# Attention pieces between scores and turnings, norm weights in the rotary table, one-hot rows for seven experts

## Chip, core and metric

The kernel runs on one core of one Trainium2 chip. The time is the device time of the program in microseconds; before the change it is 1876.73 us, the median of three runs (1873.58 to 1881.66).

## What is computed

One layer of an encoder on 1024 tokens of 1024 features, all in float32. Three branches read `h = RMSNorm(x)` through one combined projection; their merged result goes through an output projection, and a mixture of 32 experts follows.

```python
h = _rmsnorm(x, g_mix[l]); proj = h @ w_in[l]
q_a, k_a, v_a, cx, cb, cc, q_m, gate_logits = jnp.split(proj, IN_SPLITS, axis=-1)
q_a = _partial_rope(_rmsnorm(q_a.reshape(b, s, 12, 64), g_qn_attn[l]), cos, sin)   # k_a likewise
# 3 head groups of 4 heads, (window, dilation) = (128,1), (512,4), (2048,16)
#   softmax over |i - j| <= half in each strided subsequence; groups combined by their lse
z_conv = cb * conv3(cc * cx)                       # depthwise, width 3
mkv = _rmsnorm(mem, g_mem[l]) @ w_mem_kv[l]        # 256 memory tokens, 4 heads of 128
k_m = _rmsnorm(k_m, g_kn_mem[l]); o_mem = softmax(q_m k_m / sqrt(128)) v_m
merged = sum(sigmoid(gate[i]) * (branch[i] @ w_proj[i]))
x = x + merged @ w_out[l]
h2 = _rmsnorm(x, g_ffn[l])
# best of 4 expert groups, best 2 of its 8 experts: ids, weights
x = x + sum over both (silu(h2 @ w_gate[e]) * (h2 @ w_up[e])) @ w_down[e] * weight
```

The rotation turns 16 of the 64 dimensions of a head (`ROT`); the norm weights of q and k are one vector of 64 each, the same for all heads.

## The kernel before

The order of the instructions on each engine is the order in which the program is written: the kernel schedules by hand, and an engine does its instructions in that order. Products of float32 matrices are made of three matmuls (`mm3`, lines 233 to 235): both operands are kept as a rounded part and a rest, made by a copy on ScalarE and a subtraction on VectorE (`split`). Weights of the dense part stream in through SyncE's queue (`WStream`, lines 82 and 83), five raw and eight split buffers; `ws.pump()` at a unit's end splits the next block.

PSUM has three pools: `mm` with four banks (`bank()`, products and scores), `tr` with two (`trb()`, everything that is turned by TensorE), `sm` with two (`smb()`, value products `po` and small things).

**Units.** `Emit` (line 112) writes the dense part as a row of units. `E.unit(fn)` runs one, counts it, and then runs what `E.later(n, fn)` asked for n units on; `E.ahead(n, fn)` puts a step ahead of the unit that comes n later. One attention group runs in `att_group(g, before, fillers, at)`: first eight q/k units (a token tile each: 24 matmuls, then `qk_chain`), then the `before` units, then the attention units of `att_units(g)` (15, 12 and 8 in groups 0, 1 and 2) with the fillers put ahead of the units named in `at`.

`qk_chain` normalizes a q/k tile: the sum of squares, then `qn` on VectorE (line 487), the weights `gqk` on GpSimd (490), the rotation by `cs` on GpSimd (496 to 499), and three or four units later `tp()` turns it (507) and evicts four pieces, two by ScalarE and two by VectorE.

An attention unit makes its scores (737, 768 or 799), then `softmax_unit`: VectorE adds the mask and takes the maximum (698), ScalarE the exponentials (705). Its `pv()`, `PVLAG` = 2 units later, turns the probabilities (`pT_of`, 712) and copies them by ScalarE to `pTs` (714); `fin()`, one unit after that, makes the value product (751, 782, 813).

In group 0 the `before` units are those of its own v (`v_units(0)`: four units of 24 matmuls, their turnings at 565), and after the first of them `att_consts` makes the masks, after the others `mem_rows` turns the memory tokens (633; split by lines 242 and 243 into `memT`). Its fillers are the four v units of group 1. Group 1 has the v units of group 2 ahead of it and four `mem_kv` units as fillers, group 2 gate units in pieces.

**Output projection.** Sixteen units of 24 matmuls, one per token tile and half; the residual row is turned (1634) after the matmuls of `kt == 3` of the next unit, and its router logits follow after `kt == 6`.

**Experts.** Each of the 32 experts has 128 slots (`CAP`). Its weights come in four or six pieces of 1 MB through SyncE (`XStream`, 1323) and are split into `xhl` (1350 by ScalarE, 1351 by VectorE), six chunks at most ahead. A step of the loop for expert e: `gate_e` (in its middle `actT_e(e - 1)` turns the last expert's activations), `xeT(e + 1)` turns the next expert's rows (1729), `down_e(e - 1)` with the output copy `ye` by ScalarE (1789, one buffer) and the scatter that adds it to `out` by GpSimd (1790), then `up_e(e)`. `gather(e)` fetches the rows of expert e by GpSimd (1576).

Which token has which slot is known in two ways. `slot_rows(pool, e, engs)` makes eight one-hot matrices `R` (1544), and `slots(e)` multiplies them with `aux` (nine matmuls into `slots`, 1563), from which VectorE works out the row numbers `idx` (1568) and, where asked, the weights `lw`. Before the change experts 0 to 4 (`NR` = 5) have their row numbers from there, and expert 0 its weights. The others read a table: `table_put(i, c)` scatters token numbers and weights (16 puts, 1521, on GpSimd), `table_get` reads it back (four reads, 1528, on GpSimd), `table_sum` adds the copies.

```python
    for e in range(NE):
        gate_e(e)
        if e + 1 < NE: xeT(e + 1)
        if e < 2:
            slots(e + 3, weights=False); gather(e + 3)
            table_part(4 * e, 4 * e + 4)
            if e == 0: slot_rows(moe, 4, (nc.vector,))
            else: table_get()
        elif 3 <= e < NE - 3: gather(e + 3)
        if 0 < e < NE - 1:
            if e == 2: table_sum(); gather(5)
            down_e(e - 1)
        up_e(e)
        if e == 0: slots(0, rows=False)
```

## Time and profile before

| | before |
|---|---|
| median of three runs | 1876.73 us (1873.58 to 1881.66) |
| the profiled execution | 1873.2 us |
| span from its first to its last instruction | 1871.4 us |
| TensorE matmuls | 1752.9 us, 94% of the span, 8194 |
| VectorE | 962.0 us, 51% |
| ScalarE | 820.4 us, 44% |
| GpSimd | 376.9 us, 20% |
| mean granted TensorE clock | 0.969 |
| HBM read | 277.97 MB, 163 GB/s with what is written |

One execution is profiled, and all durations come from it; busy time is the time in which an engine works on an instruction, and the rest of the span it waits. The granted clock is 1 at 2.4 GHz; a mean between 0.5 and 1 is a share of the stretch at 1.2 GHz. The attention part runs from about 26 to 425 us, the rest of the dense part to 1100, the output projection to about 1225, the experts to 1860. A row of waits names the waiting instruction, what ended the wait, and total, number and longest of such waits. In a timeline row the bracket holds the engine's idle time ahead of the instruction and what released it; an entry with xN joins N instructions in a row.

### The profile page before, as it was taken

The numbers are of one execution on the slowest core, as the hardware profiler recorded it, in microseconds if no ns is written. First come the engines' busy times: TensorE is split into PE (matmuls) and PEld (weight loads), VectorE is DVE, ScalarE is ACT, GpSimd is POOL, SyncE is SP. The second block draws the span as 40 slices with busy tenths as digits, with TensorE's granted clock in tenths as the row PEclk, the third lists the DMA queues.
The fourth block names the chain that finished last, engine by engine and source line by source line (L and its number), as shares of the span: only waits on it lengthen the run. The fifth ranks groups of instructions, "written<-read, shape, count | busy, mean of one in ns | idle before, by whom it ended". The sixth has DMA issues, their size and how long they took to land.

```text
span 1871.4 us, 22857 instructions
## 1 busy us (share of the span) xinstructions
PE 1752.9 (94%) x8194; PEld 1381.9 (74%) x8194; DVE 962.0 (51%) x1985; ACT 820.4 (44%) x1459; POOL 376.9 (20%) x526
## 2 busy tenths in 40 slices
PE   5988987989999999999999999968999999999995
PEld 4765865767788888888888878755777777777774
DVE  5733644651333243122652234785777777777773
ACT  6344234243212122121442224345777777777772
POOL 6500522410100000111324110054111111112110
PEclk9999998999899999999999999968999999999998
DMA  5110022021102121122011252668899999999981
GB/s 187 36 35 24 14 70 86 15 63 30 34 18 68 34 74 46 40 62 81 1 46 52 68 199 88 226 243 294 307 358 377 357 370 359 371 372 359 371 328 20
DMA packets 99666, 289.18 MB, mean 155 GB/s; under 512 B 14448, under 2 KB 60640, under 8 KB 74848
## 3 DMA queue, kind: packets, MB, share of 16 engines
q1 hardware_dynamic: 85456, 259.03, 36.9%
q0 software_dynamic: 11904, 24.48, 5.1%
q10 hardware_dynamic: 2192, 4.20, 0.6%
q8 instruction: 65, 1.06, 0.2%
q14 instruction: 49, 0.40, 0.1%
HBM read 277.97 MB, written 26.46 MB: 163 GB/s over the span
## 4 chain that ended last, share of the span: by engine, by line
PE 68%; DVE 4%; DMA 2%; ACT 2%; issue 2%; POOL 1%; SPq 0%; POOLq 0%; ACTq 0%; DVEq 0%
PE mmb L233 19%; PE mmb L235 19%; PE mmb L234 19%; PE mmb L1784 5%; PE trb L1729 1%; PE trb L1763 1%; PE mmb L910 1%; ACT pt L705 1%; PE po L1160 1%; PE mmb L1119 1%; DMA xw<-in_w_gate_dram 1%; DVE xhl L1351 1%; PE lgp L1641 0%; DVE whl L83 0%; POOL R L1544 0%
## 5 line engine op out<-in xcount | busy, mean ns | idle before, releaser
L1351 DVE TENSOR_TENSOR xhl<-xw,xhl 128x1024 fp32r<-128x1024 f32 x320 | 377.2, 1221 | 151.0 <-ACT xhl L1350 147.4
L1350 ACT ACTIVATE xhl<-xw 128x1024 fp32r<-128x1024 f32 x320 | 328.1, 1060 | 41.9 <-PE mmb L235 33.2
L233 PE MATMUL mmb<-hT,whl 128*128 128x512 f32 x768 | 305.9, 398 | 0.0
L235 PE MATMUL mmb<-hT,whl 128*128 128x512 f32 x768 | 301.8, 393 | 0.3 <-DVE whl L83 0.2
L234 PE MATMUL mmb<-hT,whl 128*128 128x512 f32 x768 | 301.5, 393 | 0.0
L233 PE MATMUL mmb<-xhl,xT 128*128 128x512 f32 x512 | 217.7, 425 | 6.7 <-ACT xhl L1350 6.7
L83 DVE TENSOR_TENSOR whl<-wraw,whl 128x512 fp32r<-128x512 f32 (+1 forms) x196 | 135.2, 707 | 158.6 <-ACT whl L82 153.7
L235 PE MATMUL mmb<-xhl,xT 128*128 128x512 f32 x512 | 202.7, 396 | 1.4 <-DVE xT L240 1.4
L234 PE MATMUL mmb<-xhl,xT 128*128 128x512 f32 x512 | 202.8, 396 | 0.5 <-DVE xhl L1351 0.5
L233 PEld LDWEIGHTS mmb<-hT,whl 128*128 128x128 f32 x768 | 146.1, 190 | 33.7 <-issue 2.7
L235 PEld LDWEIGHTS mmb<-hT,whl 128*128 128x128 f32 x768 | 145.7, 190 | 32.4 <-DVE whl L83 1.3
L234 PEld LDWEIGHTS mmb<-hT,whl 128*128 128x128 f32 x768 | 146.1, 190 | 29.4
L82 ACT ACTIVATE whl<-wraw 128x512 fp32r<-128x512 f32 (+1 forms) x196 | 115.4, 601 | 110.8 <-PE mmb L235 88.1
L994 POOL TENSOR_TENSOR merged<-merged,sg 128x512 f32<-128x512 f32 x32 | 41.3, 1292 | 461.2 <-DVE sg L993 461.1
L233 PEld LDWEIGHTS mmb<-xhl,xT 128*128 128x128 f32 x512 | 98.6, 192 | 32.8 <-issue 7.2
L234 PEld LDWEIGHTS mmb<-xhl,xT 128*128 128x128 f32 x512 | 98.0, 191 | 27.0 <-issue 7.2
L1784 PE MATMUL mmb<-xw,aT 128*128 128x512 f32 x256 | 115.0, 592 | 0.0
L235 PEld LDWEIGHTS mmb<-xhl,xT 128*128 128x128 f32 x512 | 97.8, 191 | 23.0 <-DVE xT L240 2.1
L1576 POOL DMA_INDIRECT xe<-hbuf,idx x32 | 53.0, 1656 | 286.8 <-PE trb L1729 260.5
L233 PE MATMUL mmb<-whl,hT 128*128 128x512 f32 x256 | 106.3, 415 | 1.2 <-ACT hT L242 1.1
L993 DVE TENSOR_TENSOR sg<-mmb,sg 128x512 f32<-128x512 f32 x32 | 22.1, 690 | 165.2 <-PE mmb L235 161.5
L235 PE MATMUL mmb<-whl,hT 128*128 128x512 f32 x256 | 101.1, 395 | 0.2
(378 smaller groups left out, 2813.2 us busy)
## 6 DMA issues: line engine op xcount, KB each, us to landing
xw<-in_w_down_dram SPq DMA_DIRECT2D x64, 1024.0 KB, 12.9
xw<-in_w_gate_dram SPq DMA_DIRECT2D x62, 1024.0 KB, 18.6
xw<-in_w_up_dram SPq DMA_DIRECT2D x62, 1024.0 KB, 14.0
wraw<-in_w_in_dram SPq DMA_DIRECT2D x68, 256.0 KB, 2.9
wraw<-in_w_in_dram SPq DMA_DIRECT2D x48, 192.0 KB, 3.0
wraw<-in_w_in_dram SPq DMA_DIRECT2D x48, 128.0 KB, 2.6
xt<-in_x_dram SPq DMA_DIRECT2D x8, 512.0 KB, 6.0
wraw<-in_w_mem_kv_dram SPq DMA_DIRECT2D x16, 256.0 KB, 3.3
```

Source lines behind the costliest of these rows:

```text
L82: self.nc.scalar.activation(t[:, 0, :n], r, AF.Copy)
L83: self.nc.vector.tensor_tensor(t[:, 1, :n], r, t[:, 0, :n].bitcast(F32), OP.subtract)
L233: nc.tensor.matmul(ps, lhsT=lh, rhs=rh, start=first, stop=False)
L234: nc.tensor.matmul(ps, lhsT=lh, rhs=rl, start=False, stop=False)
L235: nc.tensor.matmul(ps, lhsT=ll, rhs=rh, start=False, stop=last)
L705: nc.scalar.activation(pt[:, c], pt[:, c], AF.Exp, bias=nb[:, h:h + 1], scale=0.125, accum_out=sg[:, qt, 1, h0 + h:h0 + h + 1])
L993: nc.vector.tensor_tensor(sg, pp, sg, OP.mult)
L994: nc.gpsimd.tensor_tensor(m_, m_, sg, OP.add)
L1350: nc.scalar.activation(t[:, 0], src, AF.Copy)
L1351: nc.vector.tensor_tensor(t[:, 1], src, t[:, 0].bitcast(F32), OP.subtract)
L1576: nc.gpsimd.indirect_dma_start(out=xe[e % 2][:CAP], out_offset=None, in_=hbuf, in_offset=bass.IndirectOffsetOnAxis(ap=slot_i(e), axis=0), ...
L1784: nc.tensor.matmul(ps[h], lhsT=t[:, a], rhs=w[:, a, h * 512:(h + 1) * 512], start=False, stop=(a == 1))
```

## The change

- `E.later` gets `first=True`, which puts a step ahead of the others that are due; `E.ahead` and `PVLAG` go. `pv()` comes four units after the scores, `fin()` two units after that and first among what is due.
- The fillers of groups 0 and 1 are cut after kt = 1, 3 and 5 into pieces of six matmuls (`CUTS4`), sixteen a group, one piece ahead of an attention unit. The turnings of group 1's v come two and four units after their piece.
- `mem_rows` leaves the v units of group 0 and becomes four fillers of its own among the attention units; `att_consts` moves to the q/k unit of tile 4.
- The norm weights of q and k: the 16 rotated dimensions are multiplied into the rotary table (`csg`, on GpSimd at the start), the others are a scale per partition (`gcol`) in the evictions behind the turning, which become one instruction each for ScalarE and VectorE. Line 490 goes; the rotation is two products over q and k for four.
- The memory keys: their squares go from GpSimd to ScalarE, the product with `y` from GpSimd to VectorE, four units later, and the weight into the eviction.
- In the output projection the turning moves from kt 3 to kt 5, the logits from 6 to 7.
- Experts 0 to 6 have row numbers and weights from one-hot rows (`NR` = 7), all made on VectorE; those for the weights of experts 0 to 2 are made a second time. The puts are spread over steps 0 to 2 (6, 6, 4), behind the gather, and the table is read in step 3 and summed in step 4.

```diff
+    def later(self, n, fn, first=False):
+
+        self.q.insert(0 if first else len(self.q), (self.t + n, fn))
...
-    def ahead(self, n, fn):
-
-        self.a.append((self.t + n, fn))
...
+            for s in range(2):
+                for c, v in ((0, n2), (1, n1)):
+                    nc.gpsimd.tensor_tensor(
+                        csg[:, s, c].rearrange("p t (a e) -> p t a e", a=2),
+                        v[:, :, None, :].to_broadcast([P, NT, 2, 8]),
+                        gqk[:, s, 0:ROT].rearrange("p (a e) -> p a e", a=2)[:, None]
+                        .to_broadcast([P, NT, 2, 8]), OP.mult)
...
+    gqk = atc.tile([P, 2, ROT], F32, name="gqk")
+    gcol = atc.tile([P, 2], F32, name="gcol")
+    for s_, g_ in ((0, g_qn_attn), (1, g_kn_attn)):
+        nc.gpsimd.dma_start(gqk[:, s_], bc_rows(g_, ROT))
+        for h in range(2):
+            nc.gpsimd.dma_start(gcol[h * HD + ROT:(h + 1) * HD, s_:s_ + 1],
+                                g_[0, ROT:HD].rearrange("(p c) -> p c", c=1))
...
-        nc.gpsimd.tensor_tensor(qv, qv, gqk[:, :, None, :].to_broadcast([P, 2, 4, HD]), OP.mult)
...
-                        nc.scalar.activation(d, src, AF.Copy)
+                    nc.scalar.activation(d, src, AF.Copy, scale=gcol[:, 0:1])
...
+                if (g, t) == (0, 4):
+                    att_consts()
...
-                        E.later(1, tp(ct, q))
+                        E.later(2 * q + 2 if cuts else q + 1, tp(ct, q))
...
-                nc.gpsimd.tensor_tensor(sq, qn, qn, OP.mult)
+                nc.scalar.activation(sq, qn.rearrange("p h d -> p (h d)"), AF.Square)
-                nc.gpsimd.tensor_tensor(qn, qn, y[:, :, None].to_broadcast([P, 4, MH]), OP.mult)
-                nc.gpsimd.tensor_tensor(qn, qn, gkm[:, None, :].to_broadcast([P, 4, MH]), OP.mult)
+                def norm():
+                    nc.vector.tensor_tensor(qn, qn, y[:, :, None].to_broadcast([P, 4, MH]), OP.mult)
...
-                    E.later(1, fin)
-                E.ahead(PVLAG[g], pv)
+                    E.later(2, fin, True)
+                E.later(4, pv)
...
-    att_group(0, [first_v(i, u) for i, u in enumerate(v_units(0))],
-              v_units(1), [2, 5, 8, 11])
-    att_group(1, v_units(2), [mem_kv(k_, m_) for k_ in ("mk", "mv") for m_ in range(2)],
-              [1, 4, 7, 10])
+    CUTS4 = (1, 3, 5)
+    f0 = flat(v_units(1, CUTS4))
+    at0 = list(range(15)) + [14]
+    for kp, i in enumerate((2, 5, 8, 11)):
+        k = at0.index(i) + 1
+        f0.insert(k, lambda kp=kp: mem_rows(kp))
+        at0.insert(k, i)
+    att_group(0, flat(v_units(0)), f0, at0)
+    f1 = flat([mem_kv(k_, m_, CUTS4) for k_ in ("mk", "mv") for m_ in range(2)])
+    att_group(1, flat(v_units(2)), f1, sorted(list(range(12)) + [1, 4, 7, 10]))
...
-                    if kt == 3 and "tp" in late:
+                    if kt == 5 and "tp" in late:
...
-    slot_rows(moe, 0, (nc.gpsimd,))
-    slot_rows(moe, 3, (nc.gpsimd,))
...
+        if e < 4:
+            slot_rows(moe, e + 3, (nc.vector,))
+        elif e < NE - 3:
+            if e == 4:
+                table_sum()
             gather(e + 3)
         if 0 < e < NE - 1:
             down_e(e - 1)
+        if e < 4:
+            slots(e + 3)
+            gather(e + 3)
+        if e < 3:
+            slot_rows(moe, e, (nc.vector,))
+            table_part(*((0, 6), (6, 12), (12, 16))[e])
         up_e(e)
+        if e < 3:
+            slots(e, rows=False)
+        elif e == 3:
+            table_get()
```

TensorE's row among the units of group 0 before: L712 turns one unit's probabilities, L737 are scores, L751 a value product, L233 to L235 the start of a filler of 24 matmuls.

```order
L751 MATMUL po_1311<-pTs_1298,vv_1065 64x128 x4
L737 MATMUL mmb_1317<-kT_664,qT_663 128x256
L737 MATMUL mmb_1318<-kT_664,qT_663 128x256
L712 MATMUL trb_1328<-ident_93,pt_1304 128x128 x4
L737 MATMUL mmb_1335<-kT_664,qT_663 128x256
L737 MATMUL mmb_1336<-kT_664,qT_663 128x256
L751 MATMUL po_1346<-pTs_1333,vv_1065 64x128 x4
L712 MATMUL trb_1352<-ident_93,pt_1321 128x128 x4
L233 MATMUL mmb_1359<-hT0_107,whl_947 128x512
L234 MATMUL mmb_1359<-hT0_107,whl_947 128x512
L235 MATMUL mmb_1359<-hT0_107,whl_947 128x512
L233 MATMUL mmb_1359<-hT1_108,whl_947 128x512
```

The same place after the change: L724 turns, L226 to L228 are a piece of a filler, L749 scores, L763 a value product.

```order
L724 MATMUL trb_1319<-ident_93,pt_1267 128x128 x4
L226 MATMUL mmb_1249<-hT4_111,whl_1019 128x512
L227 MATMUL mmb_1249<-hT4_111,whl_1019 128x512
L228 MATMUL mmb_1249<-hT4_111,whl_1019 128x512
L226 MATMUL mmb_1249<-hT5_112,whl_1019 128x512
L227 MATMUL mmb_1249<-hT5_112,whl_1019 128x512
L228 MATMUL mmb_1249<-hT5_112,whl_1019 128x512
L749 MATMUL mmb_1332<-kT_661,qT_660 128x256
L749 MATMUL mmb_1333<-kT_661,qT_660 128x256
L763 MATMUL po_1343<-pTs_1324,vv_1025 64x128 x4
L226 MATMUL mmb_1249<-hT6_113,whl_1059 128x512
L227 MATMUL mmb_1249<-hT6_113,whl_1059 128x512
```

Six matmuls stand between a turning and the next scores, and between a value product and the next turning, where turning, scores and value product stood next to each other for two units at a time.

GpSimd's row at the start of the experts before: the last four table puts (L1521), the table reads (L1528), and the first two scatters (L1790) and the gathers behind them (L1576).

```order
L1521 DMA tab_d0_89<-tsrc_7829,tdst_7830 4096x2
L1521 DMA tab_d1_90<-tsrc_7829,tdst_7830 4096x2
L1521 DMA tab_d2_91<-tsrc_7829,tdst_7830 4096x2
L1521 DMA tab_d3_92<-tsrc_7829,tdst_7830 4096x2
L1528 DMA tab_7828<-tab_d0_89 128x64
L1528 DMA tab_7828<-tab_d1_90 128x64
L1528 DMA tab_7828<-tab_d2_91 128x64
L1528 DMA tab_7828<-tab_d3_92 128x64
L1790 DMA out_0_dram<-ye_10189,idx_7825 1024x1024
L1576 DMA xe1_7820<-hbuf_87,idx2_7827 128x1024
L1790 DMA out_0_dram<-ye_10339,idx_7825 1024x1024
L1576 DMA xe0_7819<-hbuf_87,idx2_7827 128x1024
```

After the change the first two scatters are L1799, the puts L1530, the gathers L1585.

```order
L1530 DMA tab_d0_89<-tsrc_7716,tdst_7717 4096x2
L1530 DMA tab_d1_90<-tsrc_7716,tdst_7717 4096x2
L1799 DMA out_0_dram<-ye_10035,idx_7712 1024x1024
L1585 DMA xe0_7706<-hbuf_87,idx_7712 128x1024
L1530 DMA tab_d2_91<-tsrc_7716,tdst_7717 4096x2
L1530 DMA tab_d3_92<-tsrc_7716,tdst_7717 4096x2
L1530 DMA tab_d0_89<-tsrc_7716,tdst_7717 4096x2
L1530 DMA tab_d1_90<-tsrc_7716,tdst_7717 4096x2
L1530 DMA tab_d2_91<-tsrc_7716,tdst_7717 4096x2
L1530 DMA tab_d3_92<-tsrc_7716,tdst_7717 4096x2
L1799 DMA out_0_dram<-ye_10275,idx_7712 1024x1024
L1585 DMA xe1_7707<-hbuf_87,idx_7712 128x1024
```

The first scatter stands behind the first six puts where it stood behind all sixteen and the four reads; six more puts stand between it and the second.

## Rows read from the trace of the kernel before

**Rows 1.** Windows: length, busy (instructions) of PE, PEld, DVE, ACT, POOL; clock; DMA
```profile
91.00:116.00 25.00, 16.74 (x88) 13.37 (x86) 9.65 (x25) 9.29 (x20) 3.00 (x4) 0.98 0.17 35
116.00:195.00 79.00, 68.62 (x423) 48.81 (x423) 26.84 (x116) 34.31 (x97) 6.28 (x21) 0.94 0.08 24
195.00:260.00 65.00, 61.96 (x294) 50.08 (x293) 37.15 (x125) 14.16 (x37) 25.89 (x52) 1.00 0.12 37
260.00:320.00 60.00, 46.45 (x294) 33.94 (x294) 25.48 (x91) 27.94 (x79) 15.07 (x37) 0.83 0.25 75
320.00:392.00 72.00, 66.98 (x352) 53.10 (x353) 43.08 (x152) 20.08 (x53) 29.13 (x60) 0.98 0.18 53
392.00:425.00 33.00, 31.23 (x206) 20.91 (x206) 15.16 (x83) 21.28 (x80) 0.88 (x1) 1.00 0.10 26
...
1000.00:1025.00 25.00, 25.00 (x112) 20.71 (x111) 3.37 (x5) 2.94 (x5) 12.95 (x23) 1.00 0.26 68
```

**Rows 2.** Waits of TensorE, 26.5 to 425 us: total, times, longest
```profile
PE po L751 <- ACT pTs L714: 16.6, 9, 5.7
PE trb L712 <- ACT pt L705: 6.7, 10, 1.6
PE trb L565 <- DVE memT L243: 4.0, 2, 2.6
PE trb L507 <- POOL qn L499: 3.6, 1, 3.6
PE trb L507 <- DVE memT L243: 2.6, 1, 2.6
```

**Rows 3.** Timeline of one attention unit: start, duration, engine, line, [idle before, releaser]
```profile
140.62 0.70 PE L737 MATMUL mmb<-kT,qT 64*128 64x256 f32 x4
...
143.10 0.93 PE L712 MATMUL trb<-ident,pt 128*128 128x128 f32 x4 [0.36 <-ACT pt L705]
...
145.48 0.67 PE L751 MATMUL po<-pTs,vv 128*64 128x128 f32 x8 [0.82 <-ACT pTs L714]
```

**Rows 4.** Start of the experts: timelines of TensorE, ScalarE, GpSimd, VectorE; a window
```profile
1282.98 1.06 PE L1729 MATMUL trb<-ident,xe 128*128 128x128 f32 x8
...
1314.19 1.05 PE L1729 MATMUL trb<-ident,xe 128*128 128x128 f32 x8
...
1332.68 1.06 PE L1729 MATMUL trb<-ident,xe 128*128 128x128 f32 x8
...
1301.70 1.27 ACT L1789 ACTIVATE ye<-mmb,tab 128x512 f32<-128x512 f32 x2 [14.65 <-DMA out_dram<-ye,idx]
...
1290.73 1.67 POOL L1790 DMA_INDIRECT out_dram<-ye,idx  x1 [0.31 <-issue]
...
1250.80 0.16 DVE L1568 SCALAR_TENSOR_TENSOR idx<-slc 128x1 int32<-128x1 f32 x1
1250.87 1.39 DVE L1544 TENSOR_SCALAR R<-iob,pos 128x128 bf16<-128x128 bf16 x8
...
1314.20:1845.00 530.80, 530.38 (x2289) 405.46 (x2287) 390.76 (x398) 384.21 (x483) 89.10 (x54) 1.00 0.90 345
```

**Rows 5.** Timeline of ScalarE behind the turning of mem
```profile
104.25 0.84 ACT L242 ACTIVATE memT<-trb,gT 128x256 fp32r<-128x256 f32 x2 [0.79 <-DVE memT L243]
```

**Rows 6.** Timeline of GpSimd, last q/k tile of group 2
```profile
380.67 1.57 POOL L490 TENSOR_TENSOR qn<-qn,gqk 128x512 f32<-128x512 f32 x1 [2.98 <-DVE qn L487]
```

**Rows 7.** Timelines at the start: GpSimd, then VectorE
```profile
4.11 0.57 POOL L456 DMA_DIRECT2D gqk<-in_g_kn_attn_dram  x1
...
35.95 0.20 DVE L436 TENSOR_SCALAR tt<-ang 128x64 f32<-128x64 f32 x1 [0.86 <-POOL ang L434]
```

**Rows 8.** Waits of TensorE, 1100 to 1340 us
```profile
PE trb L1634 <- DVE x L1677: 6.3, 3, 2.6
...
PE slots L1563 <- POOL R L1544: 4.3, 4, 2.5
```

**Rows 9.** Line 1521, the table puts: ns min/median/max
```profile
L1521 POOL DMA_INDIRECT tab_d<-tsrc,tdst x16: 983/1099/2019, 1253.2 to 1283.5; - x16
```

More of the change, by code (lines that the diff above doesn't have):

```diff
@@ L115, in __init__ @@
         self.t = 0
-        self.q, self.a = [], []
-    def later(self, n, fn):
-        self.q.append((self.t + n, len(self.q), fn))
+        self.q = []
+    def later(self, n, fn, first=False):
+        self.q.insert(0 if first else len(self.q), (self.t + n, fn))
     def _due(self, all_=False):
         while True:
-            for k, (t, _, fn) in enumerate(self.q):
+            for k, (t, fn) in enumerate(self.q):
                 if all_ or t <= self.t:
@@ L377, in x_piece @@
         split(hT[kt][:, 0, o], hT[kt][:, 1, o], p, gT[:, 0, kt:kt + 1])
-    cs = atc.tile([P, 2, NT, 8], F32, name="cs")
+    csg = atc.tile([P, 2, 2, NT, 16], F32, name="csg")
     def rope_tables():
@@ L510, in tp @@
             for c, dst in ((0, qT[g]), (1, kT[g])):
-                for pr in range(2):
-                    src = p[:, (2 * c + pr) * P:(2 * c + pr + 1) * P].rearrange(
-                        "p (i r) -> p r i", r=dil)
-                    d = dst[:, pr].rearrange("p (r i) -> p r i", r=dil)[:, :, t * n:(t + 1) * n]
-                    if c == 0:
-                        nc.scalar.activation(d, src, AF.Copy)
-                    else:
-                        nc.vector.tensor_copy(d, src)
+                src = p[:, 2 * c * P:2 * (c + 1) * P].rearrange("p (a i r) -> p a r i", a=2, r=dil)
+                d = dst.rearrange("p a (r i) -> p a r i", r=dil)[:, :, :, t * n:(t + 1) * n]
+                if c == 0:
+                    nc.scalar.activation(d, src, AF.Copy, scale=gcol[:, 0:1])
+                else:
+                    nc.vector.tensor_scalar(d, src, gcol[:, 1:2], None, op0=OP.mult)
         lag = {NT - 2: 3, NT - 1: 4} if g == 0 else {t_: 4 for t_ in range(NT - 3, NT)}
@@ L617, in u @@
                     for q in range(2):
-                        E.later(1, tp(ct, q))
+                        E.later(2 * q + 2 if cuts else q + 1, tp(ct, q))
                 ws.pump()
-            return u
+                yield
+            g_ = gen()
+            return [lambda: next(g_)] * (len(cuts) + 1)
         return [unit(ct, hf) for ct in range(2) for hf in range(2)]
@@ L657, in u @@
                     ws.done(W[key][kt], kt % 2)
-            stg = atp.tile([P, 512], F32, name="stg", tag="stg", bufs=1)
+                if kt in cuts:
+                    yield
             r = mrs[0][:, m_:m_ + 1]
             if key == "mv":
+                stg = atp.tile([P, 512], F32, name="stg", tag="stg", bufs=1)
                 nc.scalar.activation(stg, ps, AF.Copy, scale=r)
@@ L678, in tp @@
                         nc.tensor.transpose(p[:, h * P:(h + 1) * P], qn[:, h], ident)
-                    nc.vector.tensor_copy(stg, p)
+                    nc.vector.tensor_scalar(stg, p, gkm[:, 0:1], None, op0=OP.mult)
                     nc.gpsimd.dma_start(
@@ L682, in tp @@
                         stg.rearrange("p (h m) -> p h m", h=4))
-                E.later(6, tp)
+                E.later(4, norm)
+                E.later(7, tp)
             ws.pump()
-        return u
+            yield
+        g_ = gen()
+        return [lambda: next(g_)] * (len(cuts) + 1)
     sines = rope_tables()
@@ L789, in fin @@
                         nc.vector.tensor_copy(ov[:, :, r, 0:64], pv_[:, :, 64:])
-                    E.later(1, fin)
-                E.ahead(PVLAG[g], pv)
+                    E.later(2, fin, True)
+                E.later(4, pv)
                 ws.pump()
@@ L815, in fin @@
                                               po[:, :256].rearrange("p (a i) -> p a i", a=2))
-                    E.later(1, fin)
-                E.ahead(PVLAG[g], pv)
+                    E.later(2, fin, True)
+                E.later(4, pv)
                 ws.pump()
@@ L1028, in tile_hybrid_block @@
                 E.unit(u)
-            assert not (E.q or E.a)
+            assert not E.q
         for g_ in gate_units:
@@ L1234, in tile_hybrid_block @@
     idx = post.tile([P, NR], I32, name="idx")
-    lw = post.tile([P, 1], F32, name="lw")
+    lw = post.tile([P, NR], F32, name="lw")
     idx2 = post.tile([P, NE], I32, name="idx2")
@@ L1666, in u @@
                         ws.done(W["out", hf][kt])
-                    if kt == 3 and "tp" in late:
+                    if kt == 5 and "tp" in late:
                         late["lgt"] = late.pop("tp")()
-                    if kt == 6 and "lgt" in late:
+                    if kt == 7 and "lgt" in late:
                         late.pop("lgt")()
@@ L1804, in table_part @@
     def table_part(a, b):
-        for i in range(a, b):
-            for c in range(2):
-                table_put(i, c)
+        for k in range(a, b):
+            table_put(k // 2, k % 2)
     for e in range(NE):
```

81 lines of the change are left out of this document (26 added, 55 removed).

## The prediction, made before the changed kernel ran

> **What bounds the kernel now.** I read the busy table first, then stretches of time, then who waited for whom, and single instructions only at the waits that were left. TensorE is busy for 94% of the span, so only two things can be won: stretches in which it stands still, and stretches in which its clock is granted at 1.2 instead of 2.4 GHz. Both lie in two places.
>
> The first is the attention part. Between 91 and 392 us the windows of [rows 1] give TensorE idle times of 8.3, 10.4, 3.0, 13.6 and 5.0 us (length minus PE busy), and in 392 to 425, where the third attention group runs, only 1.8. The granted clock is 0.94 and 0.83 where groups 0 and 1 run. Granted at half speed for a share of a window, the array loses (1 - clock) x length x its busy share: 79 x 0.06 x 0.87 = 4.1, 60 x 0.17 x 0.77 = 7.9, 72 x 0.02 x 0.93 = 1.3, with 0.3 for 91 to 116 makes 13.6 us. What the idle time waits for is in [rows 2]: 16.6 us for the copy of the turned probabilities (line 714), 6.7 for the exponentials (705), 4.0 + 2.6 = 6.6 behind the turning of mem (most of the 8.3 idle between 91 and 116, where the mask constants are made too), 3.6 for one q/k tile on GpSimd. One unit of group 0 is in [rows 3]: its scores start at 140.62, its turning at 143.10 and stalls for 0.36, the value product of it waits 0.82 for the copy. Two units with nothing in between cannot cover a chain of about 3 us.
>
> The second is the start of the experts. The transposes of one expert's rows follow at 18.5 us in the steady part, but 31.2 us apart at [rows 4] (1282.98, 1314.19, then 1332.68). The row of ScalarE there says why: its output copy waited 14.65 us for the scatter of the expert before, whose buffer it needs, and that scatter was issued only at 1290.73, since GpSimd's queue held 16 table puts and 4 table reads ahead of it. From the third expert's end on TensorE has no gaps.
>
> **The change part by part.**
>
> *Fillers in quarters.* Groups 0 and 1 get sixteen pieces of 6 matmuls where they had four of 24. At 25/112 = 0.223 us from start to start [rows 1] a piece is 1.34 us. A unit's scores are now followed by two pieces and parts of two other units before it is turned, 4 to 5 us against the chain of 3. What that leaves is read from group 2, which already has its fillers in such pieces ahead of its eight units: 1.77/8 = 0.22 us a unit. Group 0: 10.4 - 15 x 0.22 = 7.1 won (bounds 0 and 10.4). Group 1: 13.6 - 12 x 0.22, less 1 us for VectorE's new multiplication of the mem keys, which may wait for GpSimd: 9.9 (bounds 3 and 13).
>
> *The turning of mem and the mask constants* leave the v units: the 8.3 us idle there go, of which I leave 0.6: 7.7. The four turnings of mem land among group 0's units. Their bank is emptied by ScalarE and VectorE in strict turns ([rows 5]: the second half waited 0.79 for VectorE), and group 0's exponentials and copies queue behind that on both engines. Nothing is free there, so I price each between 0 and the longest wait seen, 2.6 [rows 2]: 4 x 1.5 = 6 lost (bounds 0 and 10.4).
>
> *q and k norm.* GpSimd loses line 490 (1.57 in [rows 6]) and half of its rotary products; only one wait hung on them, 3.6 us at 384.5. The chain gets at least 1.57 shorter, and VectorE's splits, which share the time with it, run freer: 3.0 won (bounds 1.6 and 3.6). The other 23 tiles are hidden under matmuls and give nothing. The evictions become one instruction for two on each engine, off the path.
>
> *Start.* Four more small loads stand in GpSimd's queue ahead of the rotary table, at 0.57 each [rows 7]; the table then ends up to 2.3 us later, and I take 1.8, since part of that queue stands idle for the positions. VectorE already waited 0.86 for that table, and the first q/k norm stands behind it, for which TensorE's banks wait: 1.8 lost (bounds 0 and 2.3).
>
> *Second group's v:* the turnings are spread over two units: of 3.0 idle, 1.8 won.
>
> *Clock.* Every slow stretch between 91 and 392 stands behind idle times of 2 us and more. With those gone I take 11 of the 13.6 us (bounds 4 and 13.6).
>
> Attention in sum: 7.1 + 9.9 + 7.7 - 6 + 3.0 - 1.8 + 1.8 + 11 = 32.7 us.
>
> *Output projection.* The turning and the logits move 6 and 3 matmuls later. Three waits of 6.3 us in all stood at the turning [rows 8]; the last, at the very end (2.6), stays, the other two lose up to 1.34 each: 2.5 won.
>
> *Experts.* One-hot rows of experts 0 and 3 leave GpSimd, where they held TensorE for 4.3 us [rows 8]. They don't vanish: VectorE makes those of expert 3 behind its own small routing work and the splits, 1.39 a set [rows 4], which ends some 1 us later than GpSimd did: 1 lost (bounds 3 lost and 2 won). The scatters come to stand behind six puts each instead of sixteen and the reads: at about 1.4 + 0.3 us a put these are done before the output copy is, and the 31.2 us become 18.5: 12.7 won. VectorE's load for experts 0 to 3 rises by two sets and two slot evaluations, 2 x 1.39 + 2 x 1.2 (seven or eight small instructions of 0.16), to about 20 us of an 18.5 us period (its busy time between 1314 and 1845 in [rows 4], 391 us for 28.7 periods, is 13.6 each, and waits for TensorE's slot products come on top); its splits lie some five chunks ahead, which covers most of it: 2.5 lost (bounds 0 and 5). The table read now has a whole up projection and a gate projection, 11 us, to land in; nothing waits. Sum: 12.7 - 1 - 2.5 = 9.2.
>
> On GpSimd's own speed a row and a rule differ. The 16 puts took 0.98 to 2.02 us, median 1.10, beside a VectorE busy with splits [rows 9]. The Trainium skill, page "SBUF — State Buffer", section "SBUF: two separate sides", says that a VectorE copy or tensor_scalar in a two-port mode locks GpSimd out, so that it cannot write descriptors; that speaks against making one-hot rows on VectorE just when GpSimd issues puts. By the trace's median the sum stands; by the rule it is the second rival.
>
> All together 32.7 + 2.5 + 9.2 = 44.4 us. The profiled execution took 1873.2 us (span 1871.4 and 1.8 around it), so 1828.8; the median shown is 3.5 above it, so I forecast 1832 us as a median.
>
> **Rivals.**
> 1. *The attention keeps half of its waits.* Mem's evictions and the weight splits fill ScalarE's queue, copies come late, the clock falls as before. Groups 0 and 1 win 4 and 5, mem costs 10.4, the clock gives 4: 32.7 falls to 32.7 - 3.1 - 4.9 - 4.4 - 7 = 13.3. Time 1851. For it: 16.6 us of today's waits are for ScalarE copies. Against: ScalarE is busy for under half of these windows.
> 2. *The experts' start gains nothing.* If every put takes the longest 2.02 + 0.3 us, six with a gather and a scatter of 1.67 fill 17.3 of 18.5 us of GpSimd, scatters slip again and the output copy waits as now; or VectorE's 20 us bind. Time 1832 + 9 = 1841. This is what the rule of the page would make of it.
> 3. *Better all round.* Mem's turning hides, the clock stays full, VectorE keeps up: 6 + 2.6 + 3.5 more, 1820.
> 4. *Slower, by one mechanism: the PSUM banks.* The matmul pool has four. A quartered filler holds one over three or four attention units, a unit needs two, so the next unit's scores need a bank that VectorE frees with its mask. Today no filler is open across units in groups 0 and 1. If that wait is 1.2 us in each of 27 units, groups and clock win nothing and 32 us are added: -32 + 7.7 - 6 + 3 - 1.8 + 1.8 + 11.7 gives 16 us lost, 1892. It decides from 0.6 us a unit on (16.4/27). Against it: group 2 has the same four banks with an open filler, and 0.22 us of idle a unit from all causes.
>
> That the change does not do what it says is not open for the order of the instructions, which stands above; whether GpSimd's queue drains in time is rival 2.
>
> **How the numbers follow.** Forecast 0.62; rivals 0.14, 0.12, 0.07 and 0.05. About 0.5% (9 us) is what a measurement here can tell from no change. The forecast and rivals 1 to 3 are all faster by more; with something of rival 1 and rival 2 together near the border: faster 0.92, within 0.5% 0.03, slower 0.05. The range: low end with the upper bounds of the terms (mem 6, groups 6, experts 5, start 2) not all at once, 1812; high end takes in rival 1 with rival 2, 1851 + 9 = 1860.
>
> **What the profile after would show.** Right: waits at the copy and the exponentials below 8 us in all over groups 0 and 1, clock 1.00 there; no wait of ScalarE's output copy for a scatter; spacing of the expert transposes 18.5 to 20 us from the second on; TensorE's slot wait after the first gate 4 to 7 us, now for VectorE. Wrong: waits of scores for VectorE's mask (rival 4), waits at the value products right behind each turning of mem (rival 1), puts above 2 us (rival 2). A table sum that VectorE waits for would make the last step of the experts wrong.

## The result and the profile after

The changed kernel takes 1823.13 us (median of four runs, 1822.21 to 1824.28) where the kernel before takes 1875.15 in the same comparison: ratio 0.9717, interval 0.9691 to 0.9742, 52 us less. The forecast was 1832 in a range of 1812 to 1860; the sign and the range hold, and the gain is 7 to 8 us larger than its sum of 44.4.

The page of the changed kernel: span, busy times and share of each engine.

```profile
span 1822.0 us, 22854 instructions
PE 1738.2 (95%) x8230; PEld 1373.3 (75%) x8230; DVE 965.3 (53%) x2053; ACT 821.3 (45%) x1437; POOL 330.0 (18%) x441
```

Where the 49.4 us between the two spans lie is read from marks that both kernels have in TensorE's timeline: the start of the first turning of q/k tiles in each attention group, the first matmul of the group weights, the first turning of the output projection, the matmul of the ranks, and the turnings of the rows of experts 0 and 6. The last mark is the scatter of the last expert.

| stage | before | after | moved |
|---|---|---|---|
| start to the first q/k turning | 54.2 | 54.9 | +0.7 |
| to the first q/k turning of group 1 | 151.4 | 132.3 | -19.1 |
| to that of group 2 | 144.3 | 129.3 | -15.0 |
| to the group weights | 113.9 | 108.4 | -5.5 |
| to the output projection | 645.9 | 646.0 | +0.1 |
| to the ranks | 113.3 | 117.2 | +3.9 |
| to the rows of expert 0 | 9.2 | 9.9 | +0.7 |
| to the rows of expert 6 | 118.9 | 108.4 | -10.5 |
| to the last scatter | 501.8 | 501.8 | 0 |
| to the end of the span | 18.4 | 13.8 | -4.6 |

Stretches of the changed kernel (length, busy time of PE, PEld, DVE, ACT and POOL, granted clock, DMA): the attention units of group 0, then of group 1, then of group 2. They answer to [rows 1].

```profile
105.00:163.50 58.50, 52.95 (x363) 36.69 (x361) 25.44 (x102) 35.00 (x95) 3.15 (x14) 1.00 0.10 28
237.50:291.50 54.00, 47.02 (x343) 31.99 (x340) 28.47 (x102) 30.54 (x90) 8.83 (x31) 0.97 0.30 93
357.00:391.00 34.00, 31.65 (x227) 23.00 (x226) 14.96 (x83) 20.85 (x79) 0.88 (x1) 1.00 0.12 33
```

TensorE is idle for 5.6 us in group 0 (length minus PE) where the v units and attention units of before gave away 18.6, and for 7.0 in group 1, and its clock is at 2.4 GHz but for a dip in group 1. The waits that are left between 87 and 391 us answer to [rows 2]:

```profile
PE po L763 <- ACT pTs L726: 7.0, 6, 1.6
PE mmb L226 <- ACT whl L82: 2.6, 2, 2.1
PE po L822 <- ACT pTs L726: 2.3, 3, 0.8
PE trb L508 <- POOL qn L500: 1.7, 1, 1.7
```

The 16.6 us for the copy became 7.0, and 2.3 are new in group 2, where it was 0.3; the 6.7 for the exponentials are gone, the wait for the q/k tile went from 3.6 to 1.7. New are 2.6 us in which the first mem k/v pieces wait for ScalarE's weight splits.

In the output projection two things are new, a turning at the end that waits 3.4 us, and logits that wait 1.9 for the copy ahead of them; behind the latter the clock falls. A wait of TensorE from 1070.5 to 1188.5 us, the moment of the second wait in the timeline, and the window around it:

```profile
PE trb L1643 <- DVE x L1686: 4.7, 2, 3.4
...
1116.64 1.72 PE L1650 MATMUL lgp<-wr,x1T 128*128 128x36 f32 x8 [1.91 <-ACT x1T L1645]
...
1110.00:1125.00 15.00, 13.09 (x50) 10.47 (x49) 8.74 (x18) 8.48 (x21) 0.00 (x0) 0.77 0.16 54
```

At the start of the experts the rows of experts 1 to 6 come 20.3, 19.2, 19.2, 19.2 and 19.7 us apart, where [rows 4] has one step of 31.2. The output copy and GpSimd's part of it, in the timelines of ScalarE and GpSimd:

```profile
1254.70 0.69 ACT L1798 ACTIVATE ye<-mmb,lw 128x512 f32<-128x512 f32 x1 [1.09 <-PE mmb L1793]
...
1237.33 1.61 POOL L1799 DMA_INDIRECT out_dram<-ye,idx  x1 [9.78 <-DVE pw L1559]
1239.24 5.35 POOL L1585 DMA_INDIRECT xe<-hbuf,idx  x1 [0.30 <-issue]
```

The copy of expert 1 waits for its own matmuls alone, and GpSimd stands idle for 9.8 us ahead of the scatter of expert 0.

### The profile page after: what moved, and what is told of

It reads as the page before. It is cut to its first block, busy times and chain, and to the rows that moved or that the text cites. A ratio compares the mean times of both kernels' runs of the same rounds, so it can differ in the third digit from the quotient of the medians.

```text
span 1822.0 us, 22854 instructions
## 1 busy us (share of the span) xinstructions
PE 1738.2 (95%) x8230; PEld 1373.3 (75%) x8230; DVE 965.3 (53%) x2053; ACT 821.3 (45%) x1437; POOL 330.0 (18%) x441
## 3 DMA queue, kind: packets, MB, share of 16 engines
q0 software_dynamic: 12032, 24.37, 5.1%
## 4 chain that ended last, share of the span: by engine, by line
PE 71%; DVE 5%; ACT 1%; issue 1%; DMA 1%; POOL 0%; SPq 0%; ACTq 0%; POOLq 0%; DVEq 0%
PE mmb L226 20%; PE mmb L228 20%; PE mmb L227 19%; PE mmb L1793 5%; DVE xhl L1360 2%; PE trb L1738 1%; PE trb L1772 1%; PE mmb L922 1%; PE po L1169 1%; PE mmb L1128 1%; PE lgp L1650 1%; DMA x<-in_x_dram 0%; DVE R L1553 0%; DVE whl L83 0%; DMA out_dram<-ye,idx 0%
## 5 line engine op out<-in xcount | busy, mean ns | idle before, releaser
L226 PE MATMUL mmb<-hT,whl 128*128 128x512 f32 x768 | 306.6, 399 | 0.0
L228 PE MATMUL mmb<-hT,whl 128*128 128x512 f32 x768 | 301.2, 392 | 0.0
L226 PE MATMUL mmb<-xhl,xT 128*128 128x512 f32 x512 | 215.5, 421 | 0.0
L83 DVE TENSOR_TENSOR whl<-wraw,whl 128x512 fp32r<-128x512 f32 (+1 forms) x196 | 130.9, 684 | 154.0 <-ACT whl L82 150.1
L228 PE MATMUL mmb<-xhl,xT 128*128 128x512 f32 x512 | 201.6, 394 | 0.7 <-DVE xT L233 0.7
L226 PEld LDWEIGHTS mmb<-hT,whl 128*128 128x128 f32 x768 | 145.6, 190 | 35.7 <-issue 4.0
L228 PEld LDWEIGHTS mmb<-hT,whl 128*128 128x128 f32 x768 | 145.4, 189 | 30.8
L226 PEld LDWEIGHTS mmb<-xhl,xT 128*128 128x128 f32 x512 | 97.7, 191 | 24.6 <-issue 6.5
L228 PEld LDWEIGHTS mmb<-xhl,xT 128*128 128x128 f32 x512 | 97.0, 189 | 22.2 <-DVE xT L233 1.4
L1585 POOL DMA_INDIRECT xe<-hbuf,idx x32 | 59.6, 1861 | 284.6 <-PE trb L1738 236.9
L226 PE MATMUL mmb<-whl,hT 128*128 128x512 f32 x256 | 105.7, 413 | 1.6 <-ACT hT L235 1.6
L228 PE MATMUL mmb<-whl,hT 128*128 128x512 f32 x256 | 100.4, 392 | 0.2
```

Of the source, the lines that this page charges most:

```text
L83: self.nc.vector.tensor_tensor(t[:, 1, :n], r, t[:, 0, :n].bitcast(F32), OP.subtract)
L226: nc.tensor.matmul(ps, lhsT=lh, rhs=rh, start=first, stop=False)
L228: nc.tensor.matmul(ps, lhsT=ll, rhs=rh, start=False, stop=last)
L1585: nc.gpsimd.indirect_dma_start(out=xe[e % 2][:CAP], out_offset=None, in_=hbuf, in_offset=bass.IndirectOffsetOnAxis(ap=slot_i(e), axis=0), ...
```

## The experiments

Each run is compared with runs of the kernel before on the same chip (median 1873.7 to 1875.0 us). A difference to the changed kernel's 1823.13 us goes across chips, so 2 us or less in the time alone say little; the stages, those of the table above, say more.

**e1, the attention part alone.** The changed kernel with these parts of before:

```diff
-                    if kt == 5 and "tp" in late:
+                    if kt == 3 and "tp" in late:
...
-                    if kt == 7 and "lgt" in late:
+                    if kt == 6 and "lgt" in late:
...
-NR = 7
+NR = 5
```

and the loop over the experts of before.

> The changed kernel with the output projection (turning at kt 3, logits at kt 6) and the experts of the kernel before. Theory (the stages of the two traces add up): only the attention part moved, by 38.9 us to the first matmul of the group weights, so about 1875 - 39 = 1836 us, with 113 us from the first turning of the output projection to the ranks, as before, and 31 us between the turnings of experts 3 and 4. Rival (part of the attention's gain is a clock that other stages give back, or the experts wait on something that the attention left behind): 1845 us or more.

Measured 1830.45 us, 44.0 less than before (ratio 0.977, 0.974 to 0.980). The stages are those of the changed kernel up to the output projection (132.3, 129.9, 108.4), then those of before (113.2 to the ranks, 117.8 to expert 6). Nothing is given back. The 5 us beyond the expected 39 are the last stage: 13.3 us behind the last scatter instead of 18.4.

**e2, the experts alone.** The kernel before with `NR = 7`, `lw` of seven columns and the new loop.

> The kernel before with the experts' part of the change alone. Theory: the turnings of experts 0 and 6 stand 108 to 109 us apart where they stood 119, so 10 to 11 us less, about 1865 us; no wait of the output copy for a scatter. Rival (the gain hangs on the earlier arrival of the expert weights that a shorter attention gives): under 5 us less, above 1870 us.

Measured 1866.18 us, 8.3 less (0.9957, 0.9940 to 0.9973), with 107.7 us from expert 0 to 6. The gain does not hang on the attention.

**e3, the output projection as before** in the changed kernel: the first two edits of e1.

> The changed kernel with the turning and the logits of the output projection back at kt 3 and kt 6. Theory (six matmuls between turning and logits are too few when ScalarE is late, which then also costs clock): the stage from the first turning to the ranks goes from 117.2 back to about 113.3 us, 1819 us. Rival (the low clock in that stage comes from something else, and the later turning does save part of its waits): 117 us or more, 1823 to 1826 us.

Measured 1821.10 us, 2.0 below the changed kernel, and the stage is 113.4 us instead of 117.2. The 117.2 is the long end: of the seven traces with the new places two have 117.2 us (the changed kernel and e7), with 7 us of low clock behind the wait of 1.9, and five (e5, e6, e8, e11, e12) have 115.5 or 115.6, with the same wait and 3.4 us of low clock; the seven with the old places have 112.9 to 113.5. A wait of e3, and the window that answers to 1110 to 1125 above:

```profile
PE trb L1643 <- DVE x L1686: 6.4, 3, 2.6
...
1111.30:1126.30 15.00, 13.59 (x71) 10.88 (x70) 9.17 (x20) 9.37 (x22) 0.00 (x0) 1.00 0.16 54
```

The old places wait 1.7 us more for the residual row, but nobody waits for the copy, the clock stays at 1.00, and the window holds 71 matmuls for 50.

**e4, only the order of scatter and puts**, in the kernel before:

```diff
             gather(e + 3)
-            table_part(4 * e, 4 * e + 4)
             if e == 0:
+                table_part(0, 4)
                 slot_rows(moe, 4, (nc.vector,))
-            else:
-                table_get()
...
             down_e(e - 1)
+            if e == 1:
+                table_part(4, 8)
+                table_get()
```

> The kernel before, in whose second expert step the last eight table puts and the table reads are issued behind the scatter of expert 0 instead of ahead of it; nothing else. Theory A (the scatter behind the puts is the whole loss): experts 3 and 4 come 19 us apart instead of 31, about 1863 us. Theory B (the table is then read some 10 us too late, and VectorE, which sums it, stands still with the weight splits behind it): the wait moves from the output copy to the sum, a gain of under 5 us, 1870 us or more.

Measured 1871.62 us, 2.9 less (0.9984, 0.9971 to 0.9998); experts 3 and 4 are 29.7 us apart. Waits of all engines, 1255 to 1320 us:

```profile
DVE tab L1534 <- DMA tab<-tab_d: 14.7, 1, 14.7
ACT ye L1789 <- DVE tab L1535: 14.6, 1, 14.6
```

Theory B. The scatter is now early, and the output copy waits as long as before, for the sum of the table, which holds the weight of expert 1. VectorE stands in it with the splits behind it.

**e5, mem turned in the v units again,** in the changed kernel: `mem_rows` is called behind the second, third and fourth unit of `v_units(0)`, as before, and not among the fillers.

> The changed kernel with the four turnings of mem back in the v units of group 0, as before; the mask constants stay in the q/k unit and the fillers stay in quarters. Stage from the first q/k turning to that of group 1: 132.3 us in the changed kernel. Theory of the prediction (7.7 us idle in the v units, 6 lost among the attention units): 134 us, total 1825. Rival (the turnings are nearly free among the attention units, 1 to 2 us, so all of the idle time that they cost in the v units comes back): 138 to 140 us, total 1829 to 1831.

Measured 1823.79 us, against 1823.13; stage 134.7 us, as the theory has it. But it is a trade of two large halves. Counted from the first q/k turning, the first scores of group 0 come 8.4 us later, and the units, from the first scores to the last, run 48.9 us instead of 54.9. The units of the changed kernel, then those of e5:

```profile
106.90:161.80 54.90, 49.35 (x332) 33.90 (x334) 23.67 (x97) 33.23 (x92) 3.15 (x14) 1.00 0.09 25
...
115.60:164.50 48.90, 48.62 (x319) 31.90 (x318) 20.09 (x88) 29.06 (x82) 3.09 (x14) 1.00 0.08 23
```

Without mem's turnings TensorE is idle for 0.3 us in them instead of 5.5, and the copies are waited for 0.3 us instead of 5.2.

**e6, the fillers whole,** in the changed kernel:

```diff
-    CUTS4 = (1, 3, 5)
+    CUTS4 = ()
...
-    at0 = list(range(15)) + [14]
+    at0 = [2, 5, 8, 11]
...
-                    E.later(2, fin, True)
-                E.later(4, pv)
+                    E.later(1, fin, True)
+                E.later(2, pv)
...
-    att_group(1, flat(v_units(2)), f1, sorted(list(range(12)) + [1, 4, 7, 10]))
+    att_group(1, flat(v_units(2)), f1, [1, 4, 7, 10])
```

> The changed kernel with the fillers of groups 0 and 1 uncut again (four of 24 matmuls ahead of units 2, 5, 8, 11 and 1, 4, 7, 10), value steps two and one unit later, so that lag and place are as before; mem, constants and norm weights stay as changed. Theory (the quarters are what covers the chain): both stages lose what the prediction gave them, 7.1 + 4 and 9.9 + 7 us of idle time and clock: 143 and 146 us instead of 132.3 and 129.3, total 1850. Rival (moving mem, constants and GpSimd's products is what freed ScalarE and VectorE): under 4 us each, total below 1831.

Measured 1844.78 us, 21.7 above the changed kernel. The stages say more than the sum: 149.2 (16.9 more), 133.2 (3.9 more), 110.3 (1.9 more). Waits of TensorE from 95 to 320 us:

```profile
PE po L763 <- ACT pTs L726: 12.6, 10, 4.1
PE trb L724 <- ACT pt L717: 11.2, 8, 2.4
```

Both old waits are back. But group 1 keeps 11 of its 15 us with whole fillers: group 0 goes by the theory, group 1 by the rival. Group 0's 16.9 are not the quarters alone. This run has mem's turnings among whole fillers, which the kernel before has not, and its units run 72.4 us from the first scores to the last (104.7 to 177.1), against 61.4 before and 54.9 in the changed kernel.

**e7, quarters with half the lag:** in the changed kernel `E.later(1, fin, True)` and `E.later(2, pv)`, the rest as it is.

> The changed kernel with quarters, but with the turning two steps behind the scores and the value product one behind that, where the change has four and two (a step is now a piece or a unit, so this is one attention unit of lag instead of two). Theory (a chain of 3 us needs both pieces): each of 27 units waits 1 us or more, and the clock falls with it, the two stages 150 and 145 us, total 1855 to 1870. Rival (one piece and what else stands there cover it): stages within 3 us of 132.3 and 129.3, total 1823 to 1829.

Measured 1834.63 us, 11.5 above the changed kernel, between the two theories: stages 135.7, 137.5 and 110.3. The wait for the copy is 9.1 us, that for the exponentials 2.7. One piece and one unit cover most of the chain in group 0; in group 1 they do not: its value products wait 7.2 us for the copy instead of 2.2, and the clock of that stage is 0.95 instead of 0.99.

**e8, the old norm weights** in the changed kernel: `gqk` of 64 columns, `cs`, the product on GpSimd, four evictions.

> The changed kernel with the norm weights of q and k where they were: multiplied by GpSimd into every tile, the rotation in two halves, four evictions. Theory of the prediction: the wait of the last q/k tile of group 2 comes back (3.0 us), the first turning comes 0.7 us earlier: 2 to 3 us more, 1825 to 1826 us. Rival (GpSimd and VectorE share the time, so the products also delay splits and masks in groups 0 and 1): 6 us or more, 1829 us and above, with the loss in the stages of 132.3 and 129.3 us.

Measured 1834.27 us, 11.1 above the changed kernel. The stages: 2.6, 0.9 and 4.3 us more in the attention, and 17.0 us instead of 13.8 behind the last scatter. So it is more than 6 us, but most of it does not lie where the rival put it. Part of it is the wait that was forecast, back at 3.6 us for 1.7; from 300 to 430 us the waits are this one and the copies' 2.7, 2.3 in the changed kernel:

```profile
PE trb L499 <- POOL qn L491: 3.6, 1, 3.6
PE po L815 <- ACT pTs L719: 2.7, 4, 0.8
```

**e13, the new norm weights alone** in the kernel before (with that of the memory keys as a column in its eviction).

> The kernel before with the norm weights alone: those of q and k in the rotary table and the evictions, that of the memory keys in its eviction (one product less on GpSimd for each of two tiles); nothing of the fillers, of mem, of the output projection or of the experts. Theory (what e8 lost is this part's own worth in any schedule): 9 to 11 us less, 1863 to 1866 us, with 4 us of it in the stage of group 2 and 3 to 4 us behind the last scatter (14 us instead of 17 to 18). Rival (the part is worth that only where the fillers are in quarters and ScalarE and VectorE are the limit; the prediction's 1.2 us): 1870 to 1874 us.

Measured 1865.85 us, 9.1 less than before (0.9952, 0.9937 to 0.9967). The stage of group 2 goes from 113.9 to 110.1 us, and that behind the last scatter to 13.5. It is worth about the same in either schedule; half of it lies behind the last scatter, and what changed there is in the last section. From the first q/k turning of group 2 to the group weights, before, then e13:

```profile
349.90:463.80 113.90, 108.44 (x561) 83.76 (x559) 48.35 (x186) 45.46 (x129) 24.36 (x48) 0.99 0.14 39
...
351.40:461.50 110.10, 106.66 (x562) 82.60 (x560) 46.34 (x178) 45.78 (x121) 14.61 (x29) 1.00 0.14 40
```

GpSimd's 24.4 us fall to 14.6; TensorE's idle time goes from 5.5 to 3.4 us and its busy time from 108.4 to 106.7, with the clock at 1.00 for 0.99.

**e11, all sixteen puts in the first expert step** of the changed kernel: `table_part(0, 16)` for e = 0.

> The changed kernel with all sixteen table puts in the first expert step, so that the first scatter stands behind sixteen puts again instead of six. Theory of the prediction (the number of puts ahead of it made the scatter late): it slips by ten puts of about 1.4 us, the output copy of expert 1 waits for it, up to 12 us lost, 1828 to 1835 us. Rival (without the one-hot rows in GpSimd's queue the sixteen puts are through by about the time that the output of expert 0 is there): the scatter comes 4 us later, nobody waits, within 1.5 us of 1823.

Measured 1823.63 us: the same. In GpSimd's timeline the last put is issued at 1245.06 and the scatter comes 9.0 us later than in the changed kernel, not 4; the output copy of expert 1 then waits 2.75 us for it in ScalarE's timeline, and that costs nothing that can be seen:

```profile
1246.35 1.81 POOL L1799 DMA_INDIRECT out_dram<-ye,idx  x1 [0.30 <-ACT aS L232]
...
1256.56 1.27 ACT L1798 ACTIVATE ye<-mmb,lw 128x512 f32<-128x512 f32 x2 [2.75 <-DMA out_dram<-ye,idx]
```

The sixteen puts overrun GpSimd's idle time ahead of the scatter, and 4 of the 9.0 us are a single put, of 5.37 us (the last section has such issues). But in this kernel, whose queue holds none of the 12.3 us of rows, the copy waits 2.75 us where it waited 14.65 before.

**e12, the one-hot rows of the loop on GpSimd:** `(nc.gpsimd,)` for `(nc.vector,)` in its two calls of `slot_rows`.

> The changed kernel with the seven sets of one-hot rows of the expert loop made by GpSimd instead of VectorE. Theory (a set takes GpSimd 6.1 us, two a step stand ahead of puts and scatter there): the turnings of experts 1 to 4 come 24 to 30 us apart instead of 19 to 20, total 1840 to 1860 us. Rival (VectorE is the limit at 20 us a step, and GpSimd's rows would free it): spacing 18.5 us, 1821 us.

Measured 1844.08 us, 21 more; experts 0 to 6 take 129.2 us, two steps 29.4 and 27.8. Line 1553, the rows (ns, min/median/max), and TensorE's wait for them from 1185 to 1320 us:

```profile
L1553 POOL TENSOR_SCALAR R<-iob,pos x56: 591/594/2432, 1203.4 to 1292.5; 128x128 bf16<-128x128 bf16 x56
L1553 DVE TENSOR_SCALAR R<-iob,pos x24: 241/248/521, 1189.0 to 1194.1; 128x128 bf16<-128x128 bf16 x24
...
PE slots L1572 <- POOL R L1553: 17.1, 26, 3.9
```

**e9, a better version:** the changed kernel with the output projection of e3 and

```diff
                 if kt in cuts:
+                    if key == "mk" and m_ == 0:
+                        ws.pump()
                     yield
```

> The changed kernel with the turning and logits of the output projection back at kt 3 and 6 (e3), and one weight split more behind each of the first three pieces of the first mem k/v filler. Theory (TensorE waited 2.6 us at those pieces for ScalarE's weight splits, which stood one to a unit): these waits go, stage of group 1 from 129.9 to 127 us, total 1821.1 - 2.6 = 1818.5 us. Rival (ScalarE has no room there, the splits come ahead of exponentials and copies instead): the waits move to the copies, 1821 to 1823 us.

Measured 1815.32 us (median of five, 1814.43 to 1818.36): ratio 0.9696, 0.9679 to 0.9714, 7.8 below the changed kernel and 3 below what was expected. The stage of group 1 is 125.8 us, 4.1 less than in e3 where 2.9 were expected, and the wait for the weight splits is not in its list of waits any more; the copies' wait is 7.3 us where it was 7.0. From 233 to 263 us, changed kernel, then e9:

```profile
233.00:263.00 30.00, 26.48 (x156) 17.99 (x154) 12.72 (x43) 13.19 (x36) 3.14 (x14) 0.94 0.22 69
...
233.00:263.00 30.00, 26.00 (x181) 18.45 (x180) 15.24 (x49) 17.02 (x45) 3.86 (x15) 0.98 0.26 87
```

## Why the prediction was right, and where its terms were not

**What bounds the kernel** was read rightly: idle time and clock moved, mainly in the two places named, and the 646 us ahead of the output projection (the conv, memory and gate parts) are the same to 0.1. By the stages, attention with the start gave 38.9 us for the 32.7 forecast, the output projection lost 3.9 for 2.5 won, the experts gave 9.8 for 9.2, and 4.6 came behind the last scatter, where nothing was forecast. That the sum came so near is in part luck: two errors of 6 us cancel.

**Fillers in quarters,** with their share of the clock, were put at some 11 us in group 0 and 17 in group 1, 28 in all. In group 0 the term holds: e5, with mem's turnings out of the way, runs its units in 48.9 us where they took 61.4 before, 12.5 less. In group 1 e6 gives 3.9, and the step that failed is reading all idle time of group 1 as the chain of copy and exponentials, which only the quarters would cover. Of the 11 us that the stage keeps with whole fillers, 5.9 are idle time and 5.2 busy time, with the clock at 0.97 for 0.93. One candidate for them is VectorE: in the kernel before it stood in that group for GpSimd's square of the memory keys, and the masks, for which the exponentials wait, are queued behind it. Its waits there, before (260 to 325 us), in the changed kernel (230 to 300) and in e6 (245 to 310):

```profile
DVE ssm L669 <- POOL stg L667: 6.3, 2, 3.3
...
DVE ssm L677 <- ACT sq L675: 2.3, 1, 2.3
...
DVE ssm L677 <- ACT sq L675: 5.4, 2, 3.1
```

But e6 has the 11 us with that wait nearly as long as before, so the square's move cannot be most of them. About 2 are the turnings of the v of group 2 (the "second group's v" of the prediction), spread over two units, whose waits for VectorE fell from 2.3 to 0.3 us (1.8 were forecast); up to 1.4 are the norm weights (e13). The cause of the rest is open: the order of the value products and the places of the square and its products changed together, and no run parts them.

**Mem and the mask constants:** 7.7 won and 6 lost, 1.7 net. e5 gives both halves back, 8.4 and 6.0 us, and 2.4 net in the stage; the constants stay moved there, so the 8.4 is mem's part. The reason given for the 6, that the turnings hold up the copies, is what its waits show.

**q and k norm, and the start,** were put at 3.0 and -1.8, 1.2 in all. e13 and e8 give 9.1 and 11.1. The wait fell from 3.6 to 1.7 us, as the 1.57 of line 490 in [rows 6] lets expect, with a chain that was still waited for. With the clock behind that wait, which the clock term had counted, the stage gives 3.8 to 4.3 us. Missed are 3 to 5 us behind the last scatter, which no row before the change could have told, and in e8 2.6 us in group 0, of which 2.0 are a wait of TensorE for VectorE's weight splits. The start lost nothing that can be seen: the first q/k turning stands at 54.2, 54.7, 55.0 and 56.1 us in four kernels with the old loads and at 54.5 to 55.3 in those with the new.

**Clock:** of the 13.6 us, 11 were forecast. By the same formula 54 x 0.03 x 0.87 = 1.4 us are still lost, so 12.2 came back. It is 1.00 in group 0 where [rows 1] has 0.94, 0.97 in group 1 for 0.83; the idle times of 2 us that are left there (for weight splits) are where it still dips.

**Output projection:** 2.5 won forecast; measured 3.9 lost in the profiled execution, 2.0 to 2.7 in the five traces with the shorter stretch of low clock, and 2.0 in e3's time. This step failed in its sign: it looked at the wait ahead of the turning alone ([rows 8]). With the turning at kt 5 and the logits at 7, six matmuls stand between them instead of nine, and at the change of halves ScalarE's queue holds six weight splits ahead of the copy. The sixth stood for its weights:

```profile
1115.47 0.63 ACT L82 ACTIVATE whl<-wraw 128x512 fp32r<-128x512 f32 x1 [1.31 <-DMA wraw<-in_w_out_dram]
```

In e3 the copy stands behind four splits, none of which waits. So TensorE stood for 1.9 us, and then came matmuls at 1.2 GHz. The wait at the end, of which the text said that it stays, grew from 2.6 to 3.4.

**Experts:** 9.2 forecast; 8.3 measured alone (e2), 10.5 in the stage. The three terms come out one by one: the slot wait, 4.29 us for VectorE's rows where 4.3 were waited for GpSimd's, costs nothing instead of 1; the steps of experts 2 to 6 are 0.7 to 1.2 longer than 18.5, 3.4 in all, for the forecast 2.5. But the reason for the 12.7 was half a reason. It was not the number of puts alone (e11), and not their place ahead of the scatter alone (e4): before the change the copy of expert 1 needs the scatter *and* the table, and the table stood behind 12.3 us of one-hot rows, two gathers and sixteen puts on one queue. The rows in GpSimd's timeline before, and what the late copy did to TensorE, which waited for the weight splits queued behind it on ScalarE:

```profile
1237.69 12.27 POOL L1544 TENSOR_SCALAR R<-iob,pos 128x128 bf16<-128x128 bf16 x16
...
PE mmb L233 <- ACT xhl L1350: 6.7, 1, 6.7
```

What the change has in place of it is that GpSimd makes no rows and that seven experts need no table. How much of the gain each of the two gives is not shown: no run has one without the other. e12 says only that rows on GpSimd are dear in the new loop, where TensorE waits for them directly.

**The rivals:** no scores wait for a bank that the masks free (rival 4); one value product waits 1.7 us for a bank of `sm`. Rival 1 did not come: the copies' waits went from 16.9 to 9.8 us in all three groups, with the clock restored. Its mechanism is there, as the 6 us of mem. Rival 2 by the puts' speed: the sixteen puts take 982 to 2877 ns, median 1029, against the 1099 of [rows 9], and in e2 1030; one (2.88 us; in e2 two) is above 2 us, the sign that the prediction named, and the scatters are not late. The rule of the Trainium skill, page "SBUF — State Buffer", section "SBUF: two separate sides", that VectorE in a two-port mode locks GpSimd out, is not borne out by these medians; what there is for it stands below.

## What to carry to other kernels

Cut the work that fills a gap to the size of the gap, and set the lag in those pieces: a unit's chain of mask, exponentials, turning and copy is covered by what stands between its steps, not by the sum of the fillers. When an engine's queue holds up a result, ask for everything that the result needs and not only for what the profile names as the last to come; moving the one ahead brings out the other. When a step is moved away from a wait, count again what stands between it and the next step that reads it, on the queue of the engine between them too. Before a gain is put down to a part, look for it in the stages: half of e13's lies where the part does no work.

## What the runs showed of the hardware

- Behind the last scatter there are 16.9 to 18.4 us to the end of the span in the four kernels with the old q/k norm (before, e2, e4, e8) and 13.3 to 14.0 in the ten with the new one. Most of the difference is in GpSimd's closing instructions. Its drain takes 7018 ns in all four and 3956 ns in all ten, and the instruction ahead of it (`INC_SWDGE_SEM`) 1.90 and 1.14 to 1.15 us. The drain before the change and after:

```profile
L1980 POOLq DRAIN  x3: 46/103/7018, 1863.6 to 1871.2; - x3
...
L1987 POOLq DRAIN  x3: 46/103/3956, 1817.2 to 1821.8; - x3
```

  Four small loads more stand in GpSimd's queue in the ten, and its DMA queue carries 12032 packets instead of 11904. Whether that sets the length of the drain, and why more packets would go with a shorter one, is open: no run changed it alone.
- A stall of 1.9 us of TensorE at the same place of the output projection was followed by matmuls at 1.2 GHz in all seven traces that have it, for 7 us in two and for 3.4 in five. In the seven kernels with the old places the stall there is 0.9 to 1.3 us, and the clock stayed at 2.4 GHz.
- In all nine traced kernels that make the one-hot rows of the expert loop on VectorE, two issues of GpSimd just behind such a set took 4.5 to 5.4 us (in the changed kernel the gathers at 1239.24 and 1259.56), where the others took 1.0 to 3.1. All eighteen began after the set had ended and ended 0.9 us after the four weight splits that VectorE makes behind it. With the rows on GpSimd (e12) no gather there took more than 2.13 us. But a gather at 1278.07 beside four such splits, with no set just ahead of them, took 1.40, and so it is not shown which of VectorE's instructions holds GpSimd up. TensorE waited for none of these gathers; in e11 one of the eighteen is a put, and the scatter behind it came later by it.
